# A hand-made scheduler that counts an fp32r matmul of n columns as n + 32 cycles instead of n + 6

## The chip, the core and the metric

The kernel runs on one core of one Trainium2 chip, as one launch. The metric is the device time of that launch in microseconds (us). Three runs of the kernel before gave 2651.26, 2653.59 and 2649.71 us; their median, 2651.26 us, is the time before. A difference under 0.2% (5.3 us) can't be told from no change with runs of this spread.

The engines are called as the profile calls them: PE multiplies matrices, DVE is the vector engine, ACT the scalar engine, SP issues the DMAs.

## The reference

Two transformer blocks run one after the other on 256 tokens of width 2048, all in float32:

```python
# first block
h = rms_norm(x, norm_mix)
q_a, f_a, i_a, g_a, q_b, k_b, v_b, gates = split(h @ w_in)
y_a = hgrn2_mixer(q_a, f_a, i_a, g_a, ...)            # 8 heads, recurrence in chunks of 64 tokens
y_b = chunked_relpos_attention(q_b, k_b, v_b, ...)    # 8 heads
x = x + (gate_a * (y_a @ w_proj_a) + gate_b * (y_b @ w_proj_b)) @ w_out
h = rms_norm(x, norm_ffn)
x = x + (silu(h @ w_ffn_in[:, :5632]) * (h @ w_ffn_in[:, 5632:])) @ w_ffn_out
...
# second block, steered by a vector c: shift, scale and gate rows = silu(c) @ w_ada + b_ada
h = modulate(rms_norm_2(x), shift, scale)
...                                                   # NSA heads and MoBA heads on h @ w_in_2, then w_o
x = x + gate * norm(mixed @ w_o)
...                                                   # w_up (2048 x 8192), activation, w_down, again gated
```

Nearly all arithmetic is in the products with the big weights (w_in, w_out, w_ffn_in, w_ffn_out, w_in_2, w_o, w_up, w_down), each read once. w_ada stands apart: it is multiplied with one vector only.

## The kernel before

**Tiling.** A weight comes in pairs of blocks, 256 rows by 512 columns, 512 KB by one DMA into one of 6 buffers `raw`. To reach float32 accuracy with the fp32r matmul, each pair is split: ACT writes `wh` (the fp32r copy), DVE writes `wl` = raw - wh. The splits go into a ring of a few slots. The activations are kept split in the same way (`xh`/`xl`, `hh`/`hl`, `fh`/`fl`, `uh`/`ul`). For each 128 rows of weight and each half of the tokens (tb = 0 or 1, 128 tokens), three matmuls with 512 columns add into an accumulator `acc` in PSUM: high by high, high by low, low by high. So one pair costs 12 matmuls, one ACT instruction and one DVE instruction. An accumulator that is full is read out by the group's own function (residual add, activation, gate, ...).

**What sets the order.** `Prog` is a scheduler that runs when the kernel is built. It keeps a model clock for each engine (`clk`: pe, at for ACT, dv for DVE, sp, dma). Every helper (`act`, `vec`, `mm`, `tr`, `dma`) first calls `op()`, which moves the clock of its engine by a counted duration, begun no sooner than the inputs are ready by the model, and then issues the instruction. `main()` lays down the matmul triples one after the other: before each it loads ahead (`load_ahead`), splits ahead (`split_ahead`, which goes by counts of items, not by clocks), and lets side tasks run (`pump`). A side task is a Python generator: heads of attention, norms, transposes, the w_ada product. After a step it is `due` again when the model's PE clock has reached the time at which its last step is done plus `MARGIN` = 0.2 us:

```python
t.ready = max(self.cur, self.pe) + (self.MARGIN if t.prio >= 0 else 0.0)
...
return max(t.ready, max(self.at, self.dv) - self.SLACK[t.prio])
```

So the model's clocks decide behind which triple a step is laid; on the chip each engine then runs its own instructions in that order, and waits only where data is missing.

**The w_ada product** (`gemv`, lines 1501 to 1555) runs beside the first block. Its 192 steps each load 512 KB (`graw`, 2 buffers) and make two DVE instructions on `gacc`; after every 8 steps PE transposes `gacc` (4 small matmuls). A step n is let go when `self.pe` has passed start + n * `gemv_pace` (4.5 us, line 631) and when the model says that its load has landed.

**The norms of the second block** (`norm_mod`, `norm_mod_part`, lines 1458 to 1499) stand where PE has no other work: the input of w_in_2 hangs on the last sums of w_ffn_out. For each half of the tokens and each of 4 column groups: DVE scales the residual `xr` into a buffer (`fg` or `ft`), PE transposes it into `s`, ACT or DVE applies scale and shift, ACT writes `hh`, DVE writes `hl`. Of these buffers fg is the tag of column groups 0 and 1, ft of groups 2 and 3. `ev5` (line 944) adds w_ffn_out's accumulator to `xr`.

The change touches `mm` (line 269). It is called by `emit` (all big products) and by the head tasks.

Of the kernel before, what the change touches and what calls it, by code (L numbers as in the profile page):

```python
# [99 lines left out]
class Prog:  # L100
# [168 lines left out]
    def mm(self, out, lhsT, rhs, start=True, stop=True):  # L269
        n = self.width(out)  # L270
        if lhsT.dtype == F32R:
            c = max(n + 6, 257 if n > 128 else 511)
        else:
            c = max(4 * n + 12, 1022 if n < 96 and self.width(lhsT) > 64 else 500)
        self.op("pe", c / 2400.0, [out], [lhsT, rhs])
        self.nc.tensor.matmul(out, lhsT, rhs, start=start, stop=stop)  # L276
# [1639 lines left out]
```

## Time and profile before

| | |
|---|---|
| median of 3 runs | 2651.26 us |
| profiled execution, its own time | 2654.11 us |
| span of it, first to last instruction | 2652.1 us |
| mean granted PE clock | 0.995 of 2.4 GHz |
| PE busy | 2621.3 us, 99% of the span |
| DVE busy | 1713.6 us, 65% |
| ACT busy | 1240.4 us, 47% |
| moved by DMA | 581.99 MB, mean 219 GB/s |

The profile's page gives the busy time of each engine, the span in 40 slices, the chain of work that ended last, and the costliest groups of instructions. Busy time of PE is modelled at its ends, so a shortfall is better read from the list of its waits. A time such as 1496.69 is counted from the start of the span. Around the span lie 2654.11 - 2652.1 = 2.0 us of the profiled execution.

In time, by the issue of the loads, the stages are: w_in, the first mixers and the two projections to about 640 us; w_out to about 740; w_ffn_in and w_ffn_out, in two parts each, from there to 1504, the first part of w_ffn_out beginning just after 1000; w_in_2 and the second mixers to about 1800; w_o to 1910; w_up and w_down from 1914 to the end. The w_ada product runs beside the first block, from 390 to 1305 us.

### The profile page before, as it was taken

To read this page: it belongs to the slowest core of one execution; us is meant where nothing else is said; L and a number is where in the kernel's file an instruction comes from. 1 tells how busy PE (TensorE), PEld (TensorE's weight loads), DVE (VectorE), ACT (ScalarE), POOL (GpSimd) and SP (SyncE) were. 2 spreads that over 40 slices of the span, in tenths; PEclk is the share of its full clock that TensorE was granted. 3 is DMA by queue.
4 is the path that set the end of the run, shared out by engine and by line. 5 is a ranking of instruction groups with operands and counts; after the bars stand their busy time and mean duration, and the time that the engine had idled before them with its cause. 6 is when DMAs were issued, how large, how long until landed. Compare 5 with 4: busy or idle time off the path is not lost.

```text
span 2652.1 us, 32757 instructions
## 1 busy us (share of the span) xinstructions
PE 2621.3 (99%) x12168; PEld 2166.1 (82%) x12168; DVE 1713.6 (65%) x2364; ACT 1240.4 (47%) x1756; POOL 0.2 (0%) x4
## 2 busy tenths in 40 slices
PE   9999999999999999999999999999999999999998
PEld 7888888888888888888888887888778888888887
DVE  6665668888888887788754655656554444445445
ACT  7566555444453434334443543555554444453443
POOL 0000000000000000000000000000000000000000
PEclk9999999999999999999999999999999999999999
DMA  7545448888878998888755465345355555556553
GB/s 273 184 144 169 154 168 295 292 311 307 297 290 301 324 311 293 296 309 297 259 190 196 136 218 178 126 140 184 135 177 188 197 178 196 185 182 199 182 185 131
DMA packets 163887, 581.99 MB, mean 219 GB/s; under 512 B 18448, under 2 KB 19984, under 8 KB 163472
## 3 DMA queue, kind: packets, MB, share of 16 engines
q1 hardware_dynamic: 163728, 579.91, 64.0%
q8 instruction: 95, 1.56, 0.2%
q14 instruction: 64, 0.52, 0.1%
HBM read 577.74 MB, written 2.10 MB: 219 GB/s over the span
## 4 chain that ended last, share of the span: by engine, by line
PE 91%; DVE 4%; DMA 3%; ACT 1%; issue 1%; SPq 0%; DVEq 0%; ACTq 0%
PE acc L276 84%; PE s L276 4%; PE s L281 3%; DMA graw<-in_w_ada 3%; DVE wl L232 1%; DVE gacc L236 1%; ACT wh L220 0%; PE d L276 0%; PE d L281 0%; DVE A L267 0%; ACT og L220 0%; DVE xr L236 0%; DVE ex L232 0%; DMA raw<-in_w_ffn_in 0%; DMA raw<-in_w_in 0%
## 5 line engine op out<-in xcount | busy, mean ns | idle before, releaser
L232 DVE TENSOR_TENSOR wl<-raw,wh 128x1024 fp32r<-128x1024 f32 (+2 forms) x875 | 1042.3, 1211 | 536.7 <-ACT wh L220 533.8
L220 ACT ACTIVATE wh<-raw 128x1024 fp32r<-128x1024 f32 (+2 forms) x875 | 896.7, 1047 | 611.6 <-PE acc L276 563.5
L276 PE MATMUL acc<-wh,hh 128*128 128x512 f32 (+2 forms) x1600 | 631.4, 395 | 3.9 <-ACT hh L220 3.4
L276 PE MATMUL acc<-wh,hl 128*128 128x512 f32 (+2 forms) x1600 | 619.7, 387 | 0.6 <-DVE hl L232 0.6
L276 PE MATMUL acc<-wl,hh 128*128 128x512 f32 (+2 forms) x1600 | 618.8, 387 | 1.4 <-DVE wl L232 1.4
L276 PEld LDWEIGHTS acc<-wh,hh 128*128 128x128 f32 x1600 | 301.7, 189 | 67.1 <-issue 5.2
L276 PEld LDWEIGHTS acc<-wh,hl 128*128 128x128 f32 x1600 | 301.5, 188 | 63.8 <-DVE hl L232 2.2
L276 PEld LDWEIGHTS acc<-wl,hh 128*128 128x128 f32 x1600 | 302.0, 189 | 59.0 <-DVE wl L232 2.2
L236 DVE SCALAR_TENSOR_TENSOR gacc<-graw,csilu,gacc 128x512 f32<-128x512 f32 x360 | 270.0, 750 | 68.1 <-DMA graw<-in_w_ada 60.9
L276 PE MATMUL acc<-wh,xh 128*128 128x512 f32 x704 | 282.7, 402 | 6.6 <-ACT wh L220 6.6
L276 PE MATMUL acc<-wl,xh 128*128 128x512 f32 x704 | 275.9, 392 | 0.9 <-DVE wl L232 0.9
L276 PE MATMUL acc<-wh,xl 128*128 128x512 f32 x704 | 275.9, 392 | 0.0
L276 PE MATMUL acc<-wh,uh 128*128 128x512 f32 x512 | 200.0, 391 | 0.0
L276 PE MATMUL acc<-wh,ul 128*128 128x512 f32 x512 | 199.3, 389 | 0.0
L276 PE MATMUL acc<-wl,uh 128*128 128x512 f32 x512 | 199.2, 389 | 0.0
L276 PEld LDWEIGHTS acc<-wh,xh 128*128 128x128 f32 x704 | 133.1, 189 | 32.0 <-ACT wh L220 6.5
L276 PEld LDWEIGHTS acc<-wh,xl 128*128 128x128 f32 x704 | 132.9, 189 | 28.4
L276 PEld LDWEIGHTS acc<-wl,xh 128*128 128x128 f32 x704 | 133.1, 189 | 27.8 <-DVE wl L232 2.1
L276 PE MATMUL acc<-wh,fh 128*128 128x512 f32 x320 | 125.3, 392 | 0.0
L276 PE MATMUL acc<-wh,fl 128*128 128x512 f32 x320 | 124.6, 389 | 0.0
L276 PE MATMUL acc<-wl,fh 128*128 128x512 f32 x320 | 124.5, 389 | 0.0
L276 PEld LDWEIGHTS acc<-wh,ul 128*128 128x128 f32 x512 | 96.1, 188 | 20.0
(279 smaller groups left out, 2428.8 us busy)
## 6 DMA issues: line engine op xcount, KB each, us to landing
raw<-in_w_in SPq DMA_DIRECT2D x255, 512.0 KB, 4.1
graw<-in_w_ada SPq DMA_DIRECT2D x192, 512.0 KB, 5.2
raw<-in_w_ffn_in SPq DMA_DIRECT2D x176, 512.0 KB, 5.0
raw<-in_w_up SPq DMA_DIRECT2D x128, 512.0 KB, 4.2
raw<-in_w_down SPq DMA_DIRECT2D x128, 512.0 KB, 4.2
raw<-in_w_ffn_out SPq DMA_DIRECT2D x88, 512.0 KB, 4.7
raw<-in_w_out SPq DMA_DIRECT2D x32, 512.0 KB, 5.2
raw<-in_w_o SPq DMA_DIRECT2D x32, 512.0 KB, 4.3
```

The source lines that it names most:

```text
L220: self.nc.scalar.activation(out=out, in_=in_, func=func, **kw)
L232: self.nc.vector.tensor_tensor(out=out, in0=a, in1=b, op=op)
L236: self.nc.vector.scalar_tensor_tensor(out=out, in0=a, scalar=s, in1=b, op0=op0, op1=op1)
L276: self.nc.tensor.matmul(out, lhsT, rhs, start=start, stop=stop)
L281: self.nc.tensor.transpose(out, in_, self.ident[:p, :p])
```

## The change

```diff
     def mm(self, out, lhsT, rhs, start=True, stop=True):
         n = self.width(out)
         if lhsT.dtype == F32R:
-            c = max(n + 6, 257 if n > 128 else 511)
+            c = max(n + 32, 257 if n > 128 else 511)
         else:
             c = max(4 * n + 12, 1022 if n < 96 and self.width(lhsT) > 64 else 500)
         self.op("pe", c / 2400.0, [out], [lhsT, rhs])
```

For 512 columns the model's PE clock now moves by 544 cycles (226.7 ns) in place of 518 (215.8 ns), 5% more. Matmuls of fp32 inputs (the last branch) and transposes are counted as before. No instruction's form changes; the two programs hold the same number of PE, DVE and SP instructions, and ACT has two more loads of its function table (22 against 20). What changes is the order.

From the first matmul of w_up (about 1945 us) to the end PE's order is the same in both, and so is it at the norm before w_up. The changes lie ahead of that, in three kinds of places.

**The norm ahead of w_in_2.** The engine is DVE, at the end of w_ffn_out (1491 to 1501 us in the trace before). ft_3459 and ft_3460 are column groups 2 and 3 of the first token half; hl is their low part; wl_3470 to wl_3496 are low parts of w_in_2's first pairs, in the order in which PE uses them; xr is the last residual add, and stat_73 the sum of squares that the second token half's norm begins with. Before:

```order
L232 TENSOR_TENSOR ft_3460_12078<-ft_3460_12078,modc_72 128x512
L232 TENSOR_TENSOR wl_3470_12166<-raw_3428_11969,wh_3469_12165 128x1024
L232 TENSOR_TENSOR hl_5681<-ft_3459_12077,hh_5680 128x512
L232 TENSOR_TENSOR hl_5681<-ft_3460_12078,hh_5680 128x512
L232 TENSOR_TENSOR wl_3475_12191<-raw_3433_11987,wh_3474_12190 128x1024
L232 TENSOR_TENSOR wl_3480_12197<-raw_3438_12005,wh_3479_12196 128x1024
L232 TENSOR_TENSOR wl_3485_12203<-raw_3443_12024,wh_3484_12202 128x1024
L232 TENSOR_TENSOR xr_5679<-acc_12029,xr_5679 128x512
L232 TENSOR_TENSOR wl_3490_12228<-raw_3451_12045,wh_3489_12227 128x1024
L1438 TENSOR_REDUCE stat_73<-stat_73 128x1
L241 TENSOR_SCALAR stat_73<-stat_73 128x1
L232 TENSOR_TENSOR wl_3496_12244<-raw_3456_12063,wh_3495_12243 128x1024
```

After the change, the same place:

```order
L232 TENSOR_TENSOR wl_3470_12164<-raw_3428_11971,wh_3469_12163 128x1024
L232 TENSOR_TENSOR hl_5705<-ft_3459_12079,hh_5704 128x512
L232 TENSOR_TENSOR ft_3460_12080<-ft_3460_12080,modc_72 128x512
L232 TENSOR_TENSOR wl_3475_12192<-raw_3433_11989,wh_3474_12191 128x1024
L232 TENSOR_TENSOR xr_5703<-acc_12031,xr_5703 128x512
L232 TENSOR_TENSOR hl_5705<-ft_3460_12080,hh_5704 128x512
L232 TENSOR_TENSOR wl_3480_12212<-raw_3438_12007,wh_3479_12211 128x1024
L232 TENSOR_TENSOR wl_3485_12218<-raw_3443_12026,wh_3484_12217 128x1024
L1438 TENSOR_REDUCE stat_73<-stat_73 128x1
L241 TENSOR_SCALAR stat_73<-stat_73 128x1
L232 TENSOR_TENSOR wl_3491_12234<-raw_3451_12047,wh_3490_12233 128x1024
L232 TENSOR_TENSOR wl_3496_12248<-raw_3456_12065,wh_3495_12247 128x1024
```

The second add on ft_3460 has moved from ahead of the first split to behind it and behind one hl; the residual add xr from behind four splits and two hl to behind two splits and one hl; one split has moved from ahead of the stat steps to behind them. On ACT, the copy hh of ft_3460 stands ahead of the second wh in both; three wh stand between it and the squares of xr (`fs<-xr`) where four stood, and the last wh stands behind the two stat steps instead of ahead of them. On PE only one triple has moved there.

**The end of the w_ada product.** The engine is again DVE, in the second part of w_ffn_in. Before, around wl_3069 (gacc is the running sum, graw the loaded piece of w_ada, fs and fl belong to the feed-forward part):

```order
L236 SCALAR_TENSOR_TENSOR gacc_3415<-graw_10677,csilu_74,gacc_3415 128x512 x2
L232 TENSOR_TENSOR fl_6502<-s_3066_10725,fh_6501 128x4x128
L232 TENSOR_TENSOR wl_3069_10741<-raw_3034_10612,wh_3068_10740 128x1024
L232 TENSOR_TENSOR wl_3075_10761<-raw_3039_10630,wh_3074_10760 128x1024
L236 SCALAR_TENSOR_TENSOR fs_10769<-acc_10599,stat_73,fg_3026_10594 128x512
L236 SCALAR_TENSOR_TENSOR gacc_3415<-graw_10716,csilu_74,gacc_3415 128x512 x2
```

After the change, at the same weights (wl_3071 holds what wl_3069 held):

```order
L236 SCALAR_TENSOR_TENSOR fs_10728<-acc_10587,stat_73,fg_3013_10576 128x512
L232 TENSOR_TENSOR wl_3063_10731<-raw_3030_10619,wh_3062_10730 128x1024
L232 TENSOR_TENSOR fl_6537<-s_3068_10743,fh_6536 128x4x128
L232 TENSOR_TENSOR wl_3071_10757<-raw_3039_10642,wh_3070_10756 128x1024
L232 TENSOR_TENSOR wl_3076_10775<-raw_3044_10660,wh_3075_10774 128x1024
```

The gacc steps are gone from there: they stand earlier throughout, since the model's PE clock reaches start + n * 4.5 us after fewer matmuls. In PE's order the transposes of gacc stand 9 to 189 matmuls earlier, and from the first to the last of their 24 groups lie 3519 main matmuls where 3699 lay. They are not spread evenly. Where the steps catch up after a stretch in which they were held back, successive groups of 8 steps lie 135, 132, 132, 132 and 123 main matmuls apart before, and 126, 120 and 123 after; behind it 165 and 162 apart before, 150 and 162 after.

**The heads of the first mixers.** The engine is PE, in w_in (s is a head's product, ex and lmat, lh, ll its inputs; acc are the main accumulators). Before:

```order
L276 MATMUL acc_873<-wh_276_905,xl_92 128x512
L276 MATMUL s_305_1004<-ex_928 128x128 x4
L276 MATMUL s_306_1009<-ex_933 128x128 x4
L276 MATMUL s_307_1016<-ex_928 128x128 x4
L276 MATMUL s_308_1023<-ex_933 128x128 x4
L276 MATMUL s_310_1031<-lmat_95,lh_333 128x512
```

After the change:

```order
L276 MATMUL acc_898<-wh_261_864,xl_92 128x512
L276 MATMUL s_300_989<-ex_928 128x128 x4
L276 MATMUL acc_873<-wh_276_905,xh_91 128x512
L276 MATMUL acc_873<-wl_277_906,xh_91 128x512
L276 MATMUL acc_873<-wh_276_905,xl_92 128x512
L276 MATMUL s_301_999<-ex_928 128x128 x4
L276 MATMUL s_302_1004<-ex_933 128x128 x4
L276 MATMUL s_304_1012<-lmat_95,lh_330 128x512
```

The head's products stand some triples earlier and are spread between them; over the whole of the first mixers they come up to 57 matmuls sooner, and the heads of the second block up to 30 sooner or later.

## Rows read from the trace of the kernel before

**Rows 1.** The page's head: span, and busy time of each engine with its share of the span and its instructions.

```profile
span 2652.1 us, 32757 instructions
PE 2621.3 (99%) x12168; PEld 2166.1 (82%) x12168; DVE 1713.6 (65%) x2364; ACT 1240.4 (47%) x1756; POOL 0.2 (0%) x4
```

**Rows 2.** The chain of waits in order of time, in w_up and w_down: start in us, duration in us, engine, tile, line, count of instructions.

```profile
2026.44 102.73 PE acc L276 x453
...
2204.39 102.73 PE acc L276 x453
```

**Rows 3.** The timeline of ACT and of DVE at the norm before w_up: start us, us (first start to last end of the run of instructions), instruction, forms, count.

```profile
1916.89 5.80 ACT L220 ACTIVATE wh<-raw 128x1024 fp32r<-128x1024 f32 x6
...
1920.33 5.76 DVE L232 TENSOR_TENSOR wl<-raw,wh 128x1024 fp32r<-128x1024 f32 x5
```

**Rows 4.** What PE waited for over the whole span: us in total, times, longest us.

```profile
PE acc L276 <- ACT hh L220: 3.4, 3, 1.3
PE acc L276 <- DVE wl L232: 2.3, 4, 0.8
PE s L281 <- DVE og L241: 2.2, 1, 2.2
PE s L281 <- DVE gacc L236: 2.0, 5, 0.5
PE s L281 <- DVE stat L1438: 2.0, 1, 2.0
...
PE s L276 <- DVE A L267: 0.4, 2, 0.2
```

**Rows 5.** The same list for 100 to 450 us alone (w_in and the first heads); the only other row there is the one of A above.

```profile
PE acc L276 <- DVE wl L232: 0.9, 2, 0.5
```

**Rows 6.** Timeline of DVE ahead of w_in_2; in brackets the idle time before, and what ended it.

```profile
1491.60 0.69 DVE L232 TENSOR_TENSOR ft<-ft,modc 128x512 f32<-128x512 f32 x1
1492.65 1.23 DVE L232 TENSOR_TENSOR wl<-raw,wh 128x1024 fp32r<-128x1024 f32 x1 [0.36 <-ACT wh L220]
1493.80 1.29 DVE L232 TENSOR_TENSOR hl<-ft,hh 128x512 fp32r<-128x512 f32 x2
...
1498.41 0.68 DVE L232 TENSOR_TENSOR xr<-acc,xr 128x512 f32<-128x512 f32 x1
...
1500.14 0.15 DVE L1438 TENSOR_REDUCE stat<-stat 128x1 f32<-128x4 f32 x1
...
1501.98 0.41 DVE L236 SCALAR_TENSOR_TENSOR stat<-stat 128x1 f32<-128x1 f32 x2
1502.42 0.88 DVE L241 TENSOR_SCALAR fg<-xr,stat 128x512 f32<-128x512 f32 x2
```

**Rows 7.** Timeline of ACT in the same stretch.

```profile
1492.51 1.16 ACT L220 ACTIVATE hh<-ft 128x512 fp32r<-128x512 f32 x2
1493.55 3.90 ACT L220 ACTIVATE wh<-raw 128x1024 fp32r<-128x1024 f32 x4
1499.13 0.63 ACT L220 ACTIVATE fs<-xr 128x512 f32<-128x512 f32 x1 [1.67 <-DVE xr L232]
...
1500.71 0.42 ACT L220 ACTIVATE stat<-stat 128x1 f32<-128x1 f32 x2
```

**Rows 8.** Timeline of PE in the same stretch and behind it.

```profile
1496.69 0.39 PE L276 MATMUL acc<-wh,fl 128*128 128x512 f32 x1
...
1497.14 0.39 PE L276 MATMUL acc<-wl,hh 128*128 128x512 f32 x1
...
1498.50 0.39 PE L276 MATMUL acc<-wl,hh 128*128 128x512 f32 x1
...
1502.58 0.39 PE L276 MATMUL acc<-wl,hh 128*128 128x512 f32 x1
...
1503.72 1.03 PE L281 MATMUL s<-ident,fg 128*128 128x128 f32 x8
...
1509.28 0.63 PE L276 MATMUL acc<-wh,hh 128*128 128x512 f32 x1
1509.71 0.63 PE L276 MATMUL acc<-wl,hh 128*128 128x512 f32 x1
```

**Rows 9.** Stretches, the last one the densest group of the w_ada steps in the trace: the window and its length, busy us of PE, PEld, DVE, ACT and POOL (instructions), granted PE clock, DMA's busy share, GB/s.

```profile
870.00:1000.00 130.00, 128.68 (x588) 105.81 (x587) 111.45 (x133) 50.19 (x55) 0.00 (x0) 1.00 0.91 318
1000.00:1310.00 310.00, 308.80 (x1392) 254.92 (x1391) 247.21 (x287) 123.66 (x127) 0.00 (x0) 1.00 0.84 296
...
1945.00:2640.00 695.00, 695.00 (x3136) 575.46 (x3135) 332.88 (x314) 317.10 (x371) 0.00 (x0) 1.00 0.55 183
...
967.10:997.60 30.50, 29.71 (x136) 24.07 (x135) 26.38 (x32) 9.69 (x11) 0.00 (x0) 1.00 0.90 319
```

**Rows 10.** The w_ada product in one stretch: the window, busy us of PE, PEld and DVE on the tile gacc alone (instructions), granted clock, DMA share, GB/s.

```profile
870.00:1000.00 130.00, 3.05 (x20) 2.33 (x20) 48.45 (x66) 1.00 0.91 318
```

**Rows 11.** The transposes of gacc: ns shortest/median/longest, first and last start in us, form.

```profile
L281 PE MATMUL s<-ident,gacc x96: 270/272/302, 434.8 to 1304.6; 128*128 128x128 f32 x96
```

**Rows 12.** The tile graw: who waited for it (us, times), and the time of its loads from issue to landing.

```profile
DVE gacc L236: 60.9, 47
...
DMA to landing us min/median/max: 3.4/5.2/9.8
```

## The prediction

> **What bounds the kernel now.** I read the page's head first: PE is busy for 2621.3 us of 2652.1, DVE for 65%, ACT for 47% [rows 1]. So the end is set by PE's own work and by the few microseconds for which it waits. The second view was the chain of waits: in w_up and w_down 453 matmuls take 102.73 us [rows 2], 226.8 ns each, which at 2.4 GHz is 544 cycles, that is n + 32 for 512 columns. The new count is thus the chip's pitch, and the old one, n + 6 or 518 cycles, was 5% short. The third was the timeline of ACT and DVE: six wh copies in 5.80 us and four in 3.90 [rows 3, 7] give 0.95 us each, where the model counts 1024/1200 + 0.094 = 0.947; five wl in 5.76 us and one in 1.23 [rows 3, 6] give 1.13, where it counts 1024/960 + 0.068 = 1.135. The two side engines are counted rightly. Before, therefore, PE alone ran late against the plan, and every side step that the plan put just in time had 5% of the PE time since its inputs as a hidden cushion. After, MARGIN (0.2 us) is what is left, and steps are laid fewer matmuls behind their inputs.
>
> The matmuls themselves stay; so the time can only change where PE waits. The list of its waits is short: beyond the start, acc for hh 3.4 us, for wl 2.3, s for og 2.2, gacc 2.0, stat 2.0, A 0.4 [rows 4]. All that a better plan can win is in it, and most of it stands at the norm before w_up (og, stat, part of hh and wl), where PE's order does not change. From 1945 us to 2640 PE is busy for 695.00 us of 695.00 [rows 9], with the same order in both: 0 there.
>
> **The change part by part.**
>
> *The norm ahead of w_in_2.* Here the order shows a dearer sequence. Before, the last add on ft_3460 starts at 1491.60 and ends at 1492.29, ahead of the first wl at 1492.65 [rows 6]; ACT's two hh start at 1492.51 and the next wh at 1493.55 [rows 7]. After, the add stands behind that wl (1.14 until the next can start) and one hl (0.60: two take 1.29, one 0.69). I walk it forward with these durations. The add starts at 1492.65 + 1.14 + 0.60 = 1494.39 and ends at 1495.08. The second hh on ACT then starts at 1495.1 and the second wh at 1495.65, 2.1 us later than before; it ends at 1496.70, and wl_3475 at 1497.98. PE wants it at 1497.14 [rows 8]: with 0.05 us of handing over it waits 0.9 us. The residual add xr, now next (its accumulator's last matmul starts at 1496.69 [rows 8]), starts at 1497.89, 0.5 earlier than 1498.41 [rows 6], then one hl; wl_3480 ends at 1499.09 + 1.23 = 1500.32. PE wants it at 1498.50, by then 1499.4: another 0.95. The third is in time. ACT now takes three wh (1495.65 to 1498.5), the squares of xr (0.8 with their read-out), a fourth wh to 1500.35, and the last only behind the stat steps: DVE's at 1501.4 to 1501.7, ACT's (0.42 [rows 7]) to 1502.15, wh to 1503.2, wl_3496 to 1504.5. PE wants that one at 1502.58 + 1.85 = 1504.43: 0.1 more. Sum 2.0 us. The scale steps (0.40 each on DVE, from 1502.42 [rows 6]) begin about 1504.7, and the transposes, at 1503.72 before [rows 8], need the first at 1505.7: they hide, so nothing is won back behind. Term: **+2.0**. Ends: if the earlier xr alone decided, -0.5; if PE's longer idling adds a stretch at 1.2 GHz as long as the one that the trace has behind this norm (matmuls 0.43 us apart, 1509.28 to 1509.71 [rows 8], in place of 0.227, for some 8), 1.6 more: +3.6.
>
> *The w_ada product.* It is laid by the model's PE clock. The transposes run from 434.8 to 1304.6 us [rows 11]: 184 steps in 869.8 us, 4.73 us each, which is 4.5 times 544/518. With the right count a step takes 4.5 us: the product ends some 42 us earlier and draws 5% faster on the DMA queues. In itself that hides, as DVE and DMA are not full; what counts is where steps are dense. In 870 to 1000 us there are 66 DVE instructions, 33 steps, 3.94 us each, at a DMA share of 0.91 and 318 GB/s [rows 10], and PE is idle for 1.32 us of 130 [rows 9]. The densest group, 123 matmuls, costs PE 30.50 - 29.71 = 0.8 us [rows 9]. The new order has three such groups in a row (126, 120, 123): 3 x 0.8 in place of 1.32, so +1.1. The other steps lose 1.2 us in 1000 to 1310 now (310.00 - 308.80 [rows 9]); 5% denser they may lose nothing more or twice that; I take half, +0.6. Term: **+1.7**. Ends: all gacc waits go, -2.0 [rows 4]; or the three groups are held to 3.94 us a step against the 3.71 which 29.71 us for 8 steps allow, 24 x 0.23 = 5.5, and the rest doubles its loss: +6.7.
>
> *The heads.* Up to 57 matmuls earlier in w_in. Each head step still needs its inputs from ACT and DVE, whose counts hold, plus MARGIN. PE's waits from 100 to 450 us are 0.9 for wl [rows 5] and 0.4 for A [rows 4]. A step that comes 0.2 us before its time has the next triple's 0.68 us behind it, no more. Two more loads of ACT's table (counted 1.3 us each) lie on an engine at 47%. Term: **0**; ends -1.3 (both waits go) and +2.2, one wait as long as the longest past the start [rows 4].
>
> *Norm before w_up, w_up, w_down, tail.* Same PE order; on DVE one swap of a split and a residual step there, with nothing behind them that PE wants sooner: 0.
>
> Sum: 2.0 + 1.7 + 0 = +3.7 us. Against the profiled execution's own 2654.11 (span 2652.1 and 2.0 around it) that makes 2657.8. That execution is 2.85 us above the median of the runs, 2651.26; so the predicted median is **2655.0**. The ends add to -0.5 - 2.0 - 1.3 = -3.8 and 3.6 + 6.7 + 2.2 = +12.5.
>
> The Trainium skill, "TensorE: Matmul & The Clock Gate", section "Wait — 56ns, not 53.3ns?", says that back-to-back matmuls start N/2.4 GHz + about 2.5 ns apart once warm, 215.7 ns at N = 512: it would make the old count right and speaks against the change. The trace's 226.8 ns over 906 matmuls [rows 2] disagrees, and the measurement decides.
>
> **The rivals.**
>
> *Null.* The order at the norm ahead of w_in_2 costs nothing, because ACT or DVE were further ahead than my walk has them, and the denser w_ada steps hide: 2651.3. For it: PE waits so little anywhere that the plan has cushions beyond the 5%. Against it: the walk's first delay of 2.1 us on ACT stands in the order, and DVE's splits there run one behind another. Chance 0.28.
>
> *Slower: the loads of w_ada hold DVE.* DVE takes its instructions in order, and gacc steps wait for graw 47 times, 60.9 us in all [rows 12]; a split behind such a step waits too, and PE for it. Now these waits are covered by the splits' lead. If three dense groups in a row use up the lead, PE goes at the loads' pace: +2.0 at the norm, +5.5, +1.2: 2651.3 + 8.7 = 2660.0. It decides from the point where loads (median 5.2 us, at most 9.8 [rows 12]) take longer than two steps of 3.7. Against it: 319 GB/s at a share of 0.90 [rows 9] leaves a tenth of the queues free. Chance 0.13.
>
> *Longer half clock ahead of w_in_2*: my two terms and 1.6: 2656.6. Chance 0.07.
>
> *Faster.* The exact plan removes what it can: -3.8 (the lower ends), and with PE arriving with less idling the stretch at 1.2 GHz behind the norm goes too, -1.6: 2645.9. For it: a right count is what such a scheduler wants. Against it: most of the waits stand where nothing moves, and the norm's order got worse. Chance 0.07.
>
> *The shorter pitch.* If matmuls came every 215.7 ns, the new plan would lay side steps for a PE 5% slower than it is, and the waits on just-timed steps (wl 2.3, gacc 2.0, A 0.4 [rows 4]) would at least double: 2651.3 + 4.7 = 2656.0. The pitch in the rows excludes it; chance under 0.01. The figure is that of the Trainium skill's section named above.
>
> **How the numbers follow.** The forecast has 0.45 and its own range, 2652 to 2657.5; null 0.28, the loads 0.13, the half clock 0.07, faster 0.07. A measurement here tells no change from a change only beyond 0.2%, 5.3 us: below 2646.0 and above 2656.6. Faster holds the faster case: 0.07. Slower: the loads, half of the half clock, and the forecast's upper end, 0.06: 0.22. The rest, 0.71, is within. The range leaves out the faster case and the upper half of the loads: 2648.0 to 2660.5.
>
> **What would show it.** At the norm ahead of w_in_2 PE waits for wl twice, 0.9 and 0.95 us, before its transposes of fg; xr and hh<-ft stand 0.5 earlier and 2 us later than before, relative to the matmuls. The gacc transposes end near 1262, at 4.5 us a step. In the dense groups PE's idle time is 2 to 3 us and DVE's waits for graw grow. The stretch of w_up and w_down takes 695 us unchanged. I am wrong if PE shows no wait for wl at that norm, if the DMA share in the dense groups reaches 1, or if a wait that the list of before doesn't have exceeds 2 us.

## The result and the profile after

The changed kernel takes 2674.59 us (median of 5 runs, 2667.28 to 2676.43) against 2651.26 us: a ratio of 1.0083, 95% interval 1.007 to 1.0095. It is slower by 23 us, where 2655.0 was forecast with a range to 2660.5. The profiled execution took 2676.43 us, its span is 2674.5 us.

The page's head of the changed kernel answers to [rows 1]:

```profile
span 2674.5 us, 32761 instructions
PE 2624.9 (98%) x12168; PEld 2160.1 (81%) x12168; DVE 1714.0 (64%) x2364; ACT 1244.2 (47%) x1758; POOL 0.2 (0%) x4
```

The engines have the same work. Of the 22.4 us that the span grew, 18.8 us are idle time of PE (30.8 us before, 49.6 after); its busy time, which is modelled at the ends, is 3.6 us longer for the same matmuls. What PE waits for over the whole span of the changed kernel (us in total, times, longest us) answers to [rows 4]:

```profile
PE s L281 <- DVE gacc L236: 14.1, 11, 2.0
...
PE acc L276 <- DVE wl L232: 4.8, 9, 0.8
PE acc L276 <- ACT hh L220: 3.4, 3, 1.3
PE s L281 <- DVE og L241: 2.2, 1, 2.2
PE s L281 <- DVE stat L1438: 2.0, 1, 2.0
PE s L281 <- DVE fs L236: 1.8, 4, 0.8
PE s L281 <- DVE g L232: 1.3, 3, 0.7
```

The row that has grown most, from 2.0 to 14.1 us, is the transposes of the w_ada sums; wl, fs and g add 5.1 us together. og, stat and hh stand as before.

Where the time comes from is seen by comparing the starts of the same main matmul (the first, the 150th and so on that writes acc) in the two timelines of PE. I worked these out from every start; the number of main matmuls is the same in both:

```
main matmuls         before us   after us   difference
1 to 1350               380.7      383.0       +2.3    w_in, first heads
1350 to 1500             38.8       40.6       +1.9    first steps of w_ada
1500 to 5250            883.5      903.5      +20.0    beside the w_ada product
5250 to 6000            171.9      171.9        0.0
6000 to 6300             60.6       61.6       +1.0    norm ahead of w_in_2
6300 to 7300            301.6      301.6       -0.1    second heads, w_o
7300 to 7700            113.8      111.4       -2.3    norm before w_up
7700 to the end                                 0.0    w_up, w_down
```

Below, "the stretch" means main matmuls 1500 to 5250 (426 to 1309 us before). In it PE's gaps of more than 0.25 us beyond the usual pitch sum to 3.5 us before and 21.6 us after. These 18.1 us and 1.6 us of slower matmuls behind some of the gaps make up 19.7 of the 20.0 us. The rows of the first heads and of the two norms differ almost as much between executions of one and the same order, as the part on the prediction shows.

The tile gacc (ns shortest/median/longest, first and last start in us) and, of the tile graw, who waited for it (us, times) and the time of its loads from issue to landing, all of the changed kernel, answer to [rows 11, 12]:

```profile
L281 PE MATMUL s<-ident,gacc x96: 270/272/302, 436.5 to 1284.6; 128*128 128x128 f32 x96
```

```profile
DVE gacc L236: 82.4, 65
...
DMA to landing us min/median/max: 4.1/5.3/8.4
```

The loads land as quickly as before (5.3 against 5.2 us), but DVE finds them missing 65 times instead of 47, and for 82 us instead of 61. One such place shows the mechanism. First SP's queue, then DVE, then PE in the timeline of the changed kernel (start us, us, instruction, count, in brackets the idle time before and what ended it):

```profile
1237.71 0.33 SPq L298 DMA_DIRECT2D raw<-in_w_ffn_in  x1
1238.09 0.42 SPq L298 DMA_DIRECT2D graw<-in_w_ada  x1
```

```profile
1236.46 2.36 DVE L232 TENSOR_TENSOR wl<-raw,wh 128x1024 fp32r<-128x1024 f32 x2
1240.25 1.54 DVE L236 SCALAR_TENSOR_TENSOR gacc<-graw,csilu,gacc 128x512 f32<-128x512 f32 x2 [1.43 <-DMA graw<-in_w_ada]
1241.70 1.22 DVE L232 TENSOR_TENSOR wl<-raw,wh 128x1024 fp32r<-128x1024 f32 x1
1245.20 1.54 DVE L236 SCALAR_TENSOR_TENSOR gacc<-graw,csilu,gacc 128x512 f32<-128x512 f32 x2 [2.28 <-DMA graw<-in_w_ada]
```

```profile
1244.83 0.39 PE L276 MATMUL acc<-wh,hl 128*128 128x512 f32 x1
1246.89 0.63 PE L281 MATMUL s<-ident,gacc 128*128 128x128 f32 x4 [1.67 <-DVE gacc L236]
```

SP stands in its queue at a weight load until DVE's first split (done about 1237.7) frees a raw buffer; right behind it the load of w_ada goes out at 1238.09. On DVE only two splits lie between that release and the step that uses the load. DVE is there at 1242.9 and waits 2.28 us; its sum is done at 1246.7, and PE, ready for the transposes at 1245.2, waits 1.67 us. This load took 7.0 us to land; at the median of 5.3 it would have been there at 1243.4, and DVE would still have waited 0.5 us.

### The profile page after: what moved, and what is told of

The parts are those of the page before. It is cut to its first block, busy times and chain, and to the rows that moved or that the text cites. A ratio compares the mean times of both kernels' runs of the same rounds, so it can differ in the third digit from the quotient of the medians.

```text
span 2674.5 us, 32761 instructions
## 1 busy us (share of the span) xinstructions
PE 2624.9 (98%) x12168; PEld 2160.1 (81%) x12168; DVE 1714.0 (64%) x2364; ACT 1244.2 (47%) x1758; POOL 0.2 (0%) x4
## 4 chain that ended last, share of the span: by engine, by line
PE 76%; DMA 9%; DVE 9%; issue 3%; ACT 2%; SPq 0%; DVEq 0%; ACTq 0%
PE acc L276 70%; DMA graw<-in_w_ada 8%; DVE wl L232 4%; PE s L276 4%; DVE gacc L236 3%; PE s L281 2%; ACT wh L220 1%; SPq L298 0%; DVE g L232 0%; DMA raw<-in_w_ffn_in 0%; PE d L276 0%; PE d L281 0%; DMA ident<-in_cst 0%; DMA bias<-in_rel 0%; DVE xr L236 0%
```

## The experiments

The first theories: **L**, the steps of w_ada come 4.5 instead of 4.73 us apart and the loads can't keep up; **C**, every side step has lost its cushion of 5%. The edits are in the changed kernel unless the text says the kernel before. A ratio compares with runs of the kernel before that were made beside the experiment (their medians lie between 2649.93 and 2651.87 us); in brackets stands its 95% interval. "Late loads" means loads with at most two splits of DVE between the point from which SP can issue the load and the step that uses it; it is counted in the programs' own order (a load of w_ada stands on SP behind a weight load, which needs the buffer of the weight split six earlier).

**e1: the new count only beside the w_ada product.**

```diff
-            c = max(n + 32, 257 if n > 128 else 511)
+            c = max(n + (32 if self.gq and "gemv" not in self.done else 6), 257 if n > 128 else 511)
```

> The new count n + 32 only while the w_ada product is under way, the old n + 6 before and after it. The drift between the two traces lies almost wholly between 435 and 1290 us (about +20 of +22.4 us). Theory L (the w_ada steps, laid by a right PE clock, come 4.5 instead of 4.73 us apart, which the loads of w_ada do not keep up with, so the gacc transposes make PE wait) and theory C (every just-timed step has lost its cushion of 5%, the w_ada transposes among them) both expect 2667 to 2675. A theory by which the loss comes from the heads or the two norms expects 2651 to 2656.

Measured: 2674.2 us, ratio 1.0087 (1.0072 to 1.0102). The place is right: with the new count beside the w_ada product alone, the whole loss is there. What the count costs elsewhere is small against it.

**e2: the old spacing of the steps with the new count.**

```diff
-        self.gemv_pace = 4.5
+        self.gemv_pace = 4.726
```

> The changed kernel with gemv_pace 4.726 in place of 4.5, so that the steps are as far apart in PE time as they were on the chip before. Theory L expects most of the loss back: 2650 to 2658, PE's wait for gacc under 4 us. Theory C expects the loss to stay, since the transposes still lie only 0.2 us behind their sums in a right plan: 2666 to 2675, wait for gacc above 9 us.

Measured: 2672.68 us, 1.0076 (1.0061 to 1.0091). What PE waited for, and DVE for graw:

```profile
PE s L281 <- DVE gacc L236: 8.4, 6, 4.6
...
PE s L281 <- DVE fs L236: 4.2, 5, 1.9
```

```profile
DVE gacc L236 <- DMA graw<-in_w_ada: 83.1, 63, 3.4
```

Theory L falls: the steps are planned at their old spacing and DVE still waits 83 us. The time is what theory C expected, though PE's wait for gacc, 8.4 us, lies just under the 9 that it named.

**e3: the new spacing with the old count** (the kernel before).

```diff
-        self.gemv_pace = 4.5
+        self.gemv_pace = 4.285
```

> The kernel before, count n + 6, with gemv_pace 4.285, so that on the chip the steps come 4.5 us apart as after the change. Theory L expects the loss without the change of the count: 2664 to 2674, DVE's wait for graw about 80 us. Theory C expects the kernel before: 2650 to 2656, since the cushion of 5% is still there.

Measured: 2652.24 us, 1.0003 (0.9994 to 1.0013). The waits in its trace, of PE and of DVE:

```profile
PE s L281 <- DVE gacc L236: 1.3, 1, 1.3
```

```profile
DVE gacc L236 <- DMA graw<-in_w_ada: 43.3, 33, 2.9
```

Denser steps alone cost nothing here; DVE even waits less (43 us) than in the kernel before (61). But this order also has fewer late loads, 46 instead of 67, so it does not tell spacing and late loads apart; f7 and f10 below do.

**e4: the transposes of gacc laid 2 us later.** Only the `yield` behind a sum's last step is changed; `run` takes the number as the distance from the step's end in the plan.

```diff
-                yield
+                yield (2.2,)
```

> The changed kernel with the transposes of gacc laid 2.2 us instead of 0.2 us behind the end of their sum in the plan; nothing else. Both theories have PE stand at these transposes (14.1 us in the trace of the changed kernel), so both expect PE's wait for gacc under 3 us. If that wait is the loss, 2658 to 2663; if DVE, held by the loads, makes PE wait for something else in its place (splits, fs), it stays at 2668 to 2675.

Measured: 2673.97 us, 1.0075 (1.0058 to 1.0092). PE's waits:

```profile
PE s L281 <- DVE fs L236: 8.6, 4, 3.4
...
PE s L281 <- DVE g L232: 5.2, 4, 2.9
...
PE s L281 <- DVE gacc L236: 2.6, 3, 1.6
```

The wait for gacc goes as expected and the time stays. While DVE waits for graw it does nothing else (2.28 us in the place above), so whatever PE wants next from it (fs of the feed-forward part, g of the mixers) is late in place of gacc: 13.8 us for these two. The transposes were the place where the loss was seen, not its cause; DVE's standing still is.

That led to theory **S**: the model takes 1.1 + 1.46 + 1.5 = 4.06 us from issue to landing of 512 KB (`dma`, lines 283 to 295; 0.52 MB at 360 GB/s), the trace 5.2 to 5.3. The plan lets a step go when the model's PE clock has passed that landing. 4.06 us were 18.8 matmuls by the old count and are 17.9 by the new one; as a split comes every 12 matmuls, that moves many steps from behind three splits to behind two. In the orders: 67 loads have two splits and 104 three before; 116 and 71 after. In the trace before, DVE waits 59 us in all for the loads with two splits and 6 us for those with three. Its rival **C'**: the cushion lost is that of DVE and ACT, whatever the loads do.

**e5 and h: the steps let go later than the model's landing**, by 1.2 us (e5) and 2.4 us (h).

```diff
-            self.gt[n] = self.wr[self.spans(t)[0]][0]
+            self.gt[n] = self.wr[self.spans(t)[0]][0] + 1.2
```

> The changed kernel, but a step of the w_ada product is let go only 1.2 us after the model's landing of its load (the model says about 4 us from issue to landing, the trace 5.3). Theory S: what the count decides is how many weight splits lie on DVE between the point from which SP can issue a load of w_ada and the step that uses it. Before, 67 of the 192 loads have two splits (DVE then waits, 59 us in all) and 104 have three (6 us); after, 116 have two and 71 three; and a split behind a waiting step makes PE wait. By the order of this kernel 51 have two. Theory S expects 2648 to 2655, DVE's wait for graw under 50 us. Theory C' (all steps on DVE and ACT have lost their cushion, not the loads) expects 2665 to 2675.

> The same with 2.4 us in place of 1.2: by its order 19 loads have two splits, 125 three and 43 four. Theory S expects DVE's wait for graw under 30 us and 2645 to 2654, the rest of the waits being others; theory C' expects 2665 to 2675.

Measured: e5 2657.66 us, 1.0029 (1.0018 to 1.0041); h 2653.09 us, 1.0009 (0.9999 to 1.0018). DVE's wait for graw in e5, then in h:

```profile
DVE gacc L236 <- DMA graw<-in_w_ada: 37.6, 39, 3.0
```

```profile
DVE gacc L236 <- DMA graw<-in_w_ada: 19.3, 24, 2.3
```

With the new count everywhere, the stretch takes 883.5 us in e5 and 882.3 in h, the kernel before 883.5. So the loss is undone by giving the loads time, and C' falls. e5's time is 3 us above what I expected of it; in its trace the excess lies just ahead of the stretch (main matmuls 1350 to 1500, +3.4 us) and at the norm ahead of w_in_2 (+2.3, about what the new order costs there, see below).

**g: the old count with steps let go 1.0 us earlier** (the kernel before; `- 1.0` at the same line), and **f3: every duration on ACT and DVE 5% longer in the model.**

```diff
-        end = t + dur
+        end = t + dur * (1.0 if eng == "pe" else 1.05)
```

> The kernel before, count n + 6, with its steps let go 1.0 us ahead of the model's landing: by its order 100 loads have two splits, between before (67) and after (116). Theory S expects a loss without the change of the count, in proportion 2651 + 23 x 33/49 = 2666, within 2658 to 2672. Theory C' expects 2649 to 2655, since everything else keeps its cushion.

> The changed kernel with every ACT and DVE duration in the model 5% longer, so that these engines have the old proportion to PE, and the loads have the new one. By its order 86 loads have two splits. Theory C' expects 2649 to 2656. Theory S expects the loss in part, 2651 + 23 x 19/49 = 2660, within 2655 to 2667.

Measured: g 2658.25 us, 1.0022 (1.0011 to 1.0033), DVE's waits for graw 92 us; f3 2656.51 us, 1.0018 (1.0009 to 1.0027). Late loads alone make the kernel before slower, as S says, but by 7 us, at the lower end of S's range, not by the 15 of its proportion: with DVE waiting as long as in the changed kernel (92 against 84 us), g loses only 4 us in the stretch. f3, with 86 late loads, lies within S's range and just above that of C'; its stretch takes 889.4 us. The old count seemed to give the side steps cover as well: theory **S+K**.

**f4, f5: cover by MARGIN 0.7** in place of 0.2, everywhere (f4) or beside the w_ada product alone (f5); **f2: every DMA time 5% longer in the model**; **f6: f3's edit with steps let go 1.0 us early.**

> The changed kernel with MARGIN 0.7 in place of 0.2: every side step is laid half a microsecond later behind its inputs; the loads stay as they are (103 with two splits). Theory S alone (the late loads set the loss) expects 2666 to 2675 and DVE's wait for graw about 80 us. Theory S+K (late loads cost only where PE's side steps have no cover left; the old count gave them cover) expects DVE's wait for graw still about 80 us, but PE's waits of 435 to 1310 us cut by half, 2655 to 2665.

> The changed kernel with every DMA time in the model 5% longer, so that the loads have the old proportion to PE and the rest of the plan the new one: 77 loads with two splits. Theory S alone expects 2653 to 2658, nearly all back. Theory S+K expects about half back, 2656 to 2666, since DVE and ACT have no cover.

> The changed kernel with MARGIN 0.7 only while the w_ada product is under way, 0.2 elsewhere; 120 loads with two splits. With 0.7 everywhere PE's waits of 435 to 1310 us fell from 17.6 to 9.9 us, but the first heads lost 5.7 us. Theory S+K expects 2658 to 2666; theory S alone 2668 to 2676.

> The changed kernel with every ACT and DVE duration in the model 5% longer (2656.51 us by itself) and the steps let go 1.0 us ahead of the model's landing, so that the loads come as late as in the changed kernel: 116 with two splits, as there. Theory S alone (the late loads set the loss, whatever the cover) expects 2668 to 2676 with DVE's wait for graw 80 to 95 us. Theory S+K (the loss is late loads times missing cover) expects 2657 to 2665 with the same wait.

Measured: f4 2668.65 us, 1.0077 (1.0056 to 1.0097), where the first heads alone lose 8 us against the kernel before and the stretch takes 897.0; f2 2662.27, 1.0053 (1.0037 to 1.0069); f5 2672.8, 1.0081 (1.0068 to 1.0095); f6 2672.18, 1.0076 (1.006 to 1.0091). DVE and PE in f6:

```profile
DVE gacc L236 <- DMA graw<-in_w_ada: 94.1, 74, 3.5
```

```profile
PE s L281 <- DVE gacc L236: 7.9, 9, 1.6
...
PE s L281 <- DVE fs L236: 6.2, 5, 2.0
```

f4 lies in the range of S and above that of S+K, though without the loss at the heads it would have been in the latter. f5 and f6 are the plain misses of S+K: with 119 or 120 late loads, neither a larger MARGIN nor the old proportion of DVE and ACT saves the kernel. f2 lies where S+K had it, above where S had it.

**k2, k3, k5: the loads given time, and cover added.** k2 is the kernel before with steps 2.4 us after the landing, k3 is h with MARGIN 0.7, k5 is h with MARGIN 0.7 beside the w_ada product alone.

> The kernel before, count n + 6, with the steps let go 2.4 us after the model's landing: 3 loads with two splits. Both theories expect DVE's wait for graw under 15 us and PE's waits of 435 to 1310 us near 0; they were 2.5 us, so 2646 to 2651.

> The changed kernel with the steps 2.4 us after the landing and MARGIN 0.7: 22 loads with two splits. With the landing alone 2653.09 was measured. Theory S+K expects 2648 to 2653: what is left of waits in the first block goes, the norms stay as they are; if MARGIN makes the norms later, up to 2658.

> The changed kernel with both cures in the stretch where it loses: steps let go 2.4 us after the model's landing, and MARGIN 0.7 while the w_ada product is under way. Theory S+K expects no wait of PE for gacc, fs or g from 435 to 1310 us, and with the rest as in the changed kernel 2647 to 2653, so no more than 0.1% better than the kernel before.

Measured: k2 2649.49 us, 0.9998 (0.9988 to 1.0008); k3 2656.85, 1.0032 (1.0019 to 1.0044); k5 2652.94, 1.0003 (0.9994 to 1.0012). In k2 the waits of DVE fall to this row and one of 0.2 us, and the stretch takes 880.3 us:

```profile
DVE gacc L236 <- DMA graw<-in_w_ada: 10.8, 14, 2.1
```

All three win 3 us in the stretch over the kernel before; k3 gives them back at the heads, which I had not expected (I had the norms as the risk), and no version is faster beyond what can be told.

**f7, f9, f10: count and spacing one at a time, at 101 or 102 late loads.** f7 is the kernel before with gemv_pace 4.285 and steps 1.5 us early; f9 is e2 with steps 0.3 us late; f10 is the changed kernel with steps 0.1 us late.

> New count, gemv_pace 4.726 (4.73 us a step on the chip), steps let go 0.3 us after the model's landing: 101 loads with at most two splits, as in g_old_m10 (old count, 4.73 us a step on the chip), which lost 4.1 us in the stretch of the w_ada product (887.6 against 883.5 us) and measured 2658.25. What differs is the cover of the old count alone. Theory K (cover) expects a stretch of 895 to 900 us, 2666 to 2672; theory P (dense steps on a busy DVE) expects 886 to 890, 2655 to 2661.

> Old count, gemv_pace 4.285 (4.5 us a step on the chip), steps let go 1.5 us ahead of the landing: 102 loads with two splits. Theory P expects a stretch of 895 to 900 us, 2663 to 2670; theory K expects 886 to 890, 2654 to 2660.

> New count, pace 4.5, steps let go 0.1 us after the landing: 101 loads with two splits in place of 116, nothing else. If the number of such loads sets the size of the loss, 2651 + 23 x 34/49 = 2667, and DVE's wait for graw falls from 84 to about 77 us; if these 15 loads do not matter, 2672 to 2676.

f9's stretch of 895.4 us is what theory K expected. f7's 891.3 lies between the two ranges and its time in that of K. f10 lies near the 2667 of the proportion. With g they make a square (planned us a step at the real pitch; late loads; DVE's wait for graw summed from its rows; the stretch by the starts of PE's matmuls; the median):

```
                 count  us a step  late loads  DVE waits  stretch    median  ratio (95%)
before           n+6      4.73         67         65       883.5    2651.26
e3               n+6      4.50         46         44       881.9    2652.24  1.0003 (0.9994-1.0013)
g                n+6      4.73        101         92       887.6    2658.25  1.0022 (1.0011-1.0033)
f7               n+6      4.50        102         86       891.3    2656.70  1.0016 (1.0007-1.0026)
f9               n+32     4.73        101         74       895.4    2666.29  1.0058 (1.0041-1.0075)
f10              n+32     4.50        101         70       892.6    2665.52  1.0056 (1.0041-1.0071)
e2               n+32     4.73        112         88       899.1    2672.68  1.0076 (1.0061-1.0091)
after            n+32     4.50        116         84       903.5    2674.59  1.0083 (1.0070-1.0095)
e5               n+32     4.50         51         41       883.5    2657.66  1.0029 (1.0018-1.0041)
h                n+32     4.50         19         21       882.3    2653.09  1.0009 (0.9999-1.0018)
```

The spacing has no sign of its own (g to f7 +3.7 us in the stretch, f9 to f10 -2.8). Count n + 32 in place of n + 6 at the same number of late loads adds 7.8 (g to f9) and 1.3 us (f7 to f10): a cover exists, some 5 us of the 20. The medians of the two pairs differ by 8.0 and 8.8 us, of which about 3 belong to the heads and the norm ahead of w_in_2. The rest goes with the late loads: f10 and the changed kernel differ by one number, and 15 late loads go with 10.9 us between them. That f10's 2665.5 is where the proportion had it (2667) is in part luck, since g, with as many late loads, lost 7 us where the proportion had 15. The kernels that the table leaves out fit: k2, k3 and k5, with 3, 22 and 25 late loads, take 880 to 881 us in the stretch, f2 and f3, with 77 and 86, 889, f4, with 104, 897, and f5, f6, e1 and e4, with 110 to 120, 899 to 905.

## Why the prediction was wrong

Point by point, by its own steps.

**The diagnosis held.** PE is the bound, n + 32 is the pitch, ACT and DVE were counted rightly, and the old count was a hidden cushion of 5%. What I had not asked is whether the fourth clock, the DMA's, was right too. It was not: 4.06 us in the model for a load that takes 5.2 (that median is in [rows 12]), and the short PE count made up for part of it.

**The norm ahead of w_in_2: right in mechanism and size, though this pair shows half of it.** The walk gave two waits for wl, 0.9 and 0.95 us over the usual pitch. PE's timeline of the changed kernel there:

```profile
1520.84 0.39 PE L276 MATMUL acc<-wh,hh 128*128 128x512 f32 x1
1521.84 0.50 PE L276 MATMUL acc<-wl,hh 128*128 128x512 f32 x1 [0.62 <-DVE wl L232]
...
1523.11 0.39 PE L276 MATMUL acc<-wh,hh 128*128 128x512 f32 x1
1524.18 0.50 PE L276 MATMUL acc<-wl,hh 128*128 128x512 f32 x1 [0.68 <-DVE wl L232]
...
1533.81 0.50 PE L276 MATMUL acc<-wh,hh 128*128 128x512 f32 x1 [1.25 <-ACT hh L220]
...
1535.01 0.39 PE L276 MATMUL acc<-wh,hh 128*128 128x512 f32 x1
1535.24 0.40 PE L276 MATMUL acc<-wl,hh 128*128 128x512 f32 x1
```

The two starts are 1.00 and 1.07 us apart where 0.227 is usual: 0.77 and 0.84 us lost, in the two places named. But behind the norm the matmuls are 0.23 us apart from 1535.01 on (granted clock 1.00 from 1533.8 to 1537.4 us), where before they were 0.43 apart [rows 8] (0.54 from 1507.8 to 1511.4). The wait ahead of them was the same before:

```profile
1507.83 0.62 PE L276 MATMUL acc<-wh,hh 128*128 128x512 f32 x1 [1.25 <-ACT hh L220]
```

So the stretch at 1.2 GHz is missing, and the net of this pair is +1.0, not +2.0. I had such a stretch as a possible loss of 1.6 us and as part of the rival "faster"; it went the second way. It is chance and not the order: f10 has the changed kernel's order of PE, DVE and ACT there and runs those matmuls at 1.2 GHz, and e3 has the order of before and runs them at 2.4 GHz. At the lower clock the 300 matmuls around the norm take 60.6 us before and 63.2 in f10, at the full clock 59.4 in e3 and 61.6 after the change. The order thus costs 2.2 to 2.6 us, and the +2.0 held.

**The w_ada product: this step failed.** The term was +1.7 with an upper end of +6.7; the stretch measured +20.0, and its first steps +1.9 more. The part on the dense groups was sized about right: PE waits 3.2 us for gacc and fs in them (780 to 875 us in the changed kernel), where 2 to 3 were expected. What failed is the step ahead of it, that the product in itself hides and only the dense groups count, and with it the term for the rest: "5% denser they may lose nothing more or twice that; I take half, +0.6". PE's waits from 875 to 1320 us in the changed kernel:

```profile
PE s L281 <- DVE gacc L236: 10.5, 7, 2.0
PE s L281 <- DVE fs L236: 1.6, 3, 0.8
```

That is 12.1 us behind the dense groups, where 1.2 us stood before (1000 to 1310 us); the last transposes start at 1284.6 us, not near 1262. I priced the change as denser steps, and e2, f7 and f10 show that density is not what costs. The loss goes with how many splits lie between a load and its use, which jumps in whole splits of 2.7 us and moved for 49 of 192 loads. The order that I had in hand tells that number, though not its price, before any run.

**The rival on the same place** (DVE held by the loads, 2660.0, chance 0.13) had the right chain, a load that DVE waits for and PE behind it. Its threshold was wrong: it wanted loads to take longer than two steps of 3.7 us, or the queues to be full. The loads took hardly longer than before (5.3 us against 5.2), and the DMA's share was 0.90 in the dense groups and 0.81 behind them (781.9 to 872.8 and 875 to 1320 us of the changed kernel), where most of the loss is. On room, the Trainium skill ("DMA: Bandwidth & Descriptors", section "Specifications") gives a limit of about 358 GB/s from HBM for one core. The 319 GB/s at a share of 0.90 in [rows 9] would be 354 at a full share, an estimate near that figure; no run here reaches a full share. What decides here is how long a load takes against its lead, not bandwidth.

**Heads and first norm.** Forecast 0, up to +2.2; this pair shows +2.3, but most of it belongs to this execution of the changed kernel. e2, e5, f9, f10 and h have its order of PE, DVE and ACT over the first 1300 main matmuls and take 381.2 to 381.6 us to the 1350th, where it takes 383.0; e3, f7, g and k2, with the order of before, take 379.8 to 381.4. About 0.7 us are the change's. In the trace of the changed kernel PE waits 1.0 us for the load of ident at the start, which it does in none of those five.

**Norm before w_up, w_up and w_down.** PE's order is the same, and the stretches of the changed kernel answer to [rows 9]:

```profile
1967.40:2662.40 695.00, 695.00 (x3136) 575.33 (x3135) 332.83 (x314) 317.29 (x371) 0.00 (x0) 1.00 0.55 183
```

The waits at that norm are nearly the same too, yet it is 2.3 us shorter in this pair, by the clock alone. PE in the kernel before, then in the changed one, behind the second transposes there:

```profile
1935.12 0.80 PE L276 MATMUL acc<-wh,hh 128*128 128x512 f32 x1 [1.04 <-ACT hh L220]
1935.71 0.63 PE L276 MATMUL acc<-wl,hh 128*128 128x512 f32 x1
...
1940.19 0.63 PE L276 MATMUL acc<-wh,hl 128*128 128x512 f32 x1
```

```profile
1960.09 0.50 PE L276 MATMUL acc<-wh,hh 128*128 128x512 f32 x1 [1.11 <-ACT hh L220]
```

Nearly the same idle times ahead of them are followed by matmuls at the lower clock in the one execution (granted 0.50 from 1935 to 1941.5 us) and at the full one in the other (1.00 from 1960 to 1966).

**Sum.** +2.3 + 1.9 + 20.0 + 1.0 - 0.1 - 2.3 = +22.8 by stages, where +3.7 was forecast; the +2.3 of the heads and the -2.3 at the norm before w_up belong mostly to these two executions. The error is the w_ada product: +21.9 with its first steps in place of +1.7. What stays open: why the 15 loads between 101 and 116 cost as much as the 34 between 67 and 101, and which of the old count's proportions (DMA, MARGIN, hand-over times) carries the 5 us of cover; f5 and f6 exclude MARGIN alone and ACT and DVE alone at 119 or 120 late loads.

## What to carry to other kernels

In a planner with a clock for each engine, a count that is wrong may be holding up another one: before making one clock exact, compare all of them with the trace, the DMA's issue to landing above all, and correct them together (h and k5, with both corrected, are at 1.0009 and 1.0003; that takes the loss back and wins nothing over the kernel before). Where an engine that runs in order feeds several others, moving the consumer that waits only moves the wait (e4); what must be mended is the load that the engine stands at. And before pricing a new order by density or bandwidth, count in it how much work lies between each load's release and its use.

## What the runs showed of the hardware

The clock's loss after idling differs between executions that idle alike: after 1.25 us of waiting ahead of w_in_2 the matmuls run 0.43 us apart before and 0.23 us apart after the change, and both spacings occur with either order (e3, f10). With it the norm ahead of w_in_2 takes 1.2 or 1.6 us more. The norm before w_up took 113.8 us before and in k2, and 110.7 to 111.8 in e3, g and f7, which have the same order of PE, DVE and ACT there; the clock and the waits both differ. So 1 to 3 us at such a place differ between executions, and a term of that size can't be forecast from the order.

The loads of w_ada, 512 KB each, land 4.9 to 5.3 us after their issue (median) in every kernel here, whatever the spacing, at a DMA share of 0.83 to 0.87 from 430 to 1260 us; the shortest took 3.1 us.
